# One step of a hybrid attention and matrix-memory layer on one core: stores issued from another DMA queue, and a longer way from fetch to cast

## The chip, the cores and the metric

The kernel runs on one core of one Trainium2 chip. The metric is the device time of one execution in microseconds (us); lower is better. The engines are TensorE (PE in the profile, with PEld for its weight loads), VectorE (DVE), ScalarE (ACT), GpSimd (POOL) and SyncE (SP), which here only issues transfers. A transfer (DMA) is an instruction in the queue of the engine that issues it: that engine waits for what the transfer needs, issues it and goes on. The kernel before issues from SyncE (SPq in the profile) and from ScalarE (ACTq).

## What is computed

One layer of a streaming encoder for two groups that share the weights: a prompt of 2048 rows and a sample group of 8 x 16 rows, 1024 wide, all in float32. Cut from the reference:

```python
h = rms_norm(x, norm_g[0])
z = h @ w_in
qa, ka, va, qb, kb, vb, ob, ib, fb = jnp.split(z, IN_SPLITS, axis=-1)
att = band_attention(qa, ka, va)      # 8 heads x 64; own chunk of 64 and 8 before, relative bias
att = rms_norm(att, g_att)
hb, (c1, n1, m1) = mlstm_sequence(qh, kh, vh, ig, lf, c0, n0, m0)   # 4 heads x 128, matrix memory
mlstm_out = head_rms_norm(hb) * g_mlstm * sigmoid(ob)
x = x + rms_norm(jnp.concatenate([att, mlstm_out], -1) @ w_out, norm_g[1])
u = rms_norm(x, norm_g[2]) @ w_up     # then a causal convolution of width 3, gelu(gate) * up
x = x + rms_norm(g @ w_down, norm_g[3])
```

The sample group attends to a cache of 512 keys and values and starts its matrix memory from a given state for each of its 8 sequences. Outputs are the rows and the new caches and states.

## The kernel before, in words

Every large product is made of three passes (`mm3`, lines 93 to 97): each float32 operand is split into a high part (a cast on ScalarE) and a low part (a subtraction on VectorE), and high x high, high x low and low x high are summed.

The kernel has two phases. In the **mixers' phase** TensorE works through the columns of `w_in` in 28 groups, 14 for each half of the prompt. ScalarE copies each result from TensorE's accumulators to a staging tile (L224, L226) and issues its store to DRAM (L239, L275). Between the pieces of this projection the work of the two mixers is woven in. At the end of the phase `project` (from L962) takes the mixed rows tile by tile through `w_out`, normalises them and adds the input. The **ConvFFN phase** follows, in three blocks of rows.

*How the weaving works.* Attention and matrix memory are streams of small generators, called units. A `Pipe` holds one stream: each call of `step` starts the next unit and moves every unit that is under way by one `yield`. `pump`, called after each piece of the projection with what that piece costs TensorE and VectorE, steps the two pipes in turn, at most two steps a call, until the planned VectorE time has caught up with a set share of the planned TensorE time. A `yield 0.0, 0.0` is a step without cost, and `bubble()` is an empty unit: it lets one step pass in which nothing new starts. So the distance in steps between two parts of a unit sets how much other work lies between them. From this order of emission, the framework fixes when the kernel is built in which order each engine gets its instructions and puts in all waits.

*The attention stream.* `load_head` (L321) fetches the bias, queries (L334) and keys (L337) of one head and one group of 512 rows into `raw` tiles, of which there are three; one step later it casts queries (L342) and keys (L346) and fetches the values (L351), and a step after that casts those (L355). Four `att_unit`s use them. `att_stream` starts the fetch of the next head ahead of the four units of the present one. Where it starts afresh (at the beginning, after the bias has been built, after each part of the sample group's attention) it starts the fetch, lets two empty units pass and then the fetch of the next head. At the end of a pair of heads `att_unit` stores 512 rows x 128 columns to `mixd` (L440).

*The matrix memory.* `prep_prompt` and `prep_sample` work out the gates; they store the running maxima (`md`, L582 and L623) and decays (`dd`, L583 and L624) to DRAM and load the decays back, broadcast (L585, L626). `mlstm` goes through a head in pairs of 128-row chunks; `finish_heads` (L633) ends a pair and stores it to `mixd` or `mixs` (L655), with two small GpSimd operations (L646, L647) in its middle. `mlstm_sample` takes the 8 states of a head two at a time: `batches` loads two (L769), prepares masked queries on GpSimd (`qz`, L771 and L774), multiplies (`cus`, L781 and L782), updates the states in place and stores them (L787). The tiles of these states share two buffers with the results that L655 stores, so a load waits until the store from two tiles before has landed.

*The sample group's attention* fetches keys (L847) and values (L897) of each sequence, GpSimd copies the own keys beside the cached ones (L848), ScalarE casts (L852, L901); the result goes to `atts` (L911). `project` ends each tile with an addition on GpSimd (L1027) and the store of `x2d` (L1028). GpSimd also masks the decay rows (L673), sets two corners of the bias (L326, L327) and takes square roots (L84).

Of the kernel before, what the change touches and what calls it, by code (L numbers as in the profile page):

```python
# [17 lines left out]
P = 128  # L18
# [26 lines left out]
def hymba_step(ctx: ExitStack, tc: tile.TileContext, I: dict, O: dict):  # L45
# [116 lines left out]
    def bubble():  # L162
        return iter([])
# [157 lines left out]
    def load_head(s):  # L321
        pair, kg, hh, h, nm = s.pair, s.kg, s.hh, s.h, s.nm
        if kg % 2 == 0:
            nb = pa.tile([P, 640], F32, tag="nb", name=f"nb{nm}", bufs=2)
            nc.sync.dma_start(nb, bias_src(h, P, 640))
            nc.gpsimd.memset(nb[0:64, 576:640], BIG)  # L326
            nc.gpsimd.memset(nb[64:128, 0:64], BIG)  # L327
            nbs[hh] = nb
        s.nb = nbs[hh]
        rows = slice(hh * 64, hh * 64 + 64)  # L330
        qr = raw_tile(f"qraw{nm}")[:, :512]
        krs = [raw_tile(f"kraw{nm}_{g}")[:, :512] for g in s.segs]
        for r in range(2):
            nc.sync.dma_start(qr[r * 64:r * 64 + 64, :], qTd[pair][kg][rows, :])  # L334
        for kr, g in zip(krs, s.segs):
            for r in range(2):
                nc.sync.dma_start(kr[r * 64:r * 64 + 64, :], kTd[pair][g][rows, :])  # L337
        yield 0.0, 0.0
        s.kh = pa.tile([P, 1024], F32R, tag="kh", name=f"kh{nm}", bufs=2)
        s.kl = pa.tile([P, 1024], F32R, tag="kl", name=f"kl{nm}", bufs=2)  # L340
        s.qs = pa.tile([P, 512], F32R, tag="qs", name=f"qs{nm}", bufs=2)
        nc.scalar.copy(s.qs, qr)  # L342
        nc.vector.tensor_tensor(s.qs[64:128], qr[64:128], s.qs[64:128], op=ALU.subtract)
        for si, kr in enumerate(krs):
            c = slice(si * 512, (si + 1) * 512)
            nc.scalar.copy(s.kh[:, c], kr)  # L346
            nc.vector.tensor_tensor(s.kl[:, c], kr, s.kh[:, c], op=ALU.subtract)
        new = [g for g in s.segs if g == kg or (h, g) not in vhl]
        vrs = [raw_tile(f"vraw{nm}_{g}")[:, :4 * DA].rearrange("p (a d) -> p a d", a=4) for g in new]
        for vr, g in zip(vrs, new):  # L350
            nc.sync.dma_start(vr, vd[h // 4][g][:, :, (h % 4) * DA:(h % 4 + 1) * DA])  # L351
        yield 0.0, 0.6 + 0.6 * len(krs)
        for vr, g in zip(vrs, new):
            t = pa.tile([P, 4, P], F32R, tag="vhl", name=f"vhl{nm}_{g}", bufs=4)
            nc.scalar.copy(t[:, :, 0:DA], vr)  # L355
            nc.vector.tensor_tensor(t[:, :, DA:P], vr, t[:, :, 0:DA], op=ALU.subtract)
            vhl[h, g] = t
        s.v = {g: vhl[h, g] for g in s.segs}
        if kg % 2:
            for g in s.segs:  # L360
                vhl.pop((h, g))
        yield 0.0, 0.34 * len(new)

    def att_unit(s, g2, j):
# [68 lines left out]
        for jj in range(4):  # L433
# [3 lines left out]
            st.rearrange("p a (h d) -> p a h d", h=2),  # L437
            ao.rearrange("p (a h d) -> p a h d", a=4, h=2),
            rinv.unsqueeze(3).broadcast_to([P, 4, 2, DA]), op=ALU.mult)
        nc.sync.dma_start(mixd[kg][:, :, pair * P:(pair + 1) * P], st)  # L440
        yield 0.43, 0.7

    def att_stream():

        ready = None
        while True:
            if ready is None:
                if not heads:
                    yield None
                    continue  # L450
                item = heads.popleft()
                if callable(item):
                    yield FLUSH
                    yield from item()
                    continue
                ready = item
                yield load_head(ready)
                yield bubble()
                yield bubble()
            cur, ready = ready, None  # L460
            if heads and not callable(heads[0]):
                ready = heads.popleft()
                yield load_head(ready)
            for g2 in range(2):
                for j in range(2):
                    yield att_unit(cur, g2, j)
# [80 lines left out]
    def prep_prompt(half):  # L547
        n = 8
        ig, lf, nlf = log_gates(1 + 8 * half, n, f"p{half}")
        f2 = lambda t: t.rearrange("p c h -> p (c h)")  # L550
        yield 0.3, 0.8
        a, b = cum_rows(f2(ig), f2(lf), f2(nlf), 32, tri, f"p{half}")
        ca = pm.tile([P, P], F32, tag="kw", name=f"cm{half}", bufs=2)[:32, :]
        nc.vector.tensor_tensor_scan(ca, a, a, NEG, op0=ALU.max, op1=ALU.max)
        yield 0.3, 0.4
        rt = ps_sm(f"rt{half}")
        transpose(rt[0:1, 0:32], ca[:, P - 1:P], 32)
        transpose(rt[0:1, 32:64], b[:, P - 1:P], 32)
        row = pm.tile([1, 2, n, HB], F32, tag="rowl", name=f"rowl{half}", bufs=1)
        nc.vector.tensor_copy(row.rearrange("p a c h -> p (a c h)"), rt[0:1, 0:64])  # L560
        o = 8 * half
        for h in range(HB):
            nc.vector.tensor_tensor_scan(mrow[:, o + 1:o + 9, h], row[:, 0, :, h], row[:, 1, :, h],
                                         mrow[:, o:o + 1, h], op0=ALU.max, op1=ALU.add)
        yield 0.3, 0.5
        mp = ps_sm(f"mp{half}")
        transpose(mp[0:32, 0:1], mrow[:, o:o + 8, :].rearrange("p c h -> p (c h)"), 1)
        mprev = small.tile([32, 1], F32, tag="mprev", name=f"mprev{half}")
        nc.vector.tensor_copy(mprev, mp[0:32, 0:1])
        yield 0.3, 0.8  # L570
        pk = pm.tile([P, P], F32, tag="kw", name=f"pk{half}", bufs=2)
        nc.vector.tensor_scalar(ca, ca, mprev, None, op0=ALU.max)
        nml = small.tile([32, 1], F32, tag="nml", name=f"nml{half}")
        nc.vector.tensor_scalar(nml, ca[:, P - 1:P], -1.0, None, op0=ALU.mult)
        nc.vector.tensor_copy(pk[0:32, :], a)
        nc.scalar.activation(pk[32:64, :], ca, AF.Exp, bias=mprev, scale=-1.0)
        nc.vector.tensor_tensor(b, b, ca, op=ALU.add)
        nc.scalar.activation(pk[64:96, :], b, AF.Exp, scale=-1.0)
        nc.scalar.activation(pk[96:128, :], a, AF.Exp, bias=nml)
        md = dt_([32, P], f"md{half}")  # L580
        dd = dt_([32, 1], f"dd{half}")
        nc.sync.dma_start(md, ca)  # L582
        nc.sync.dma_start(dd, pk[32:64, P - 1:P])  # L583
        dec = pm.tile([P, n, HB], F32, tag="dec", name=f"dec{half}", bufs=1)
        nc.sync.dma_start(dec, dd.rearrange("(c h) o -> o c h", c=n).broadcast_to([P, n, HB]))  # L585
        yield 0.0, 0.8
        cols = pack_columns(pk, "p")
        stab[half] = (md, dec, cols)
        yield 0.3, 0.8

    def prep_sample():
# [8 lines left out]
        a, b = cum_rows(f2(ig), f2(lf), f2(nlf), HB, trib, "s")  # L600
        yield 0.3, 0.8
        ms = small.tile([HB, DB], F32, tag="mss", name="mss")
        nc.sync.dma_start(ms, I["state_m"])
        ca = pm.tile([P, P], F32, tag="kw", name="cms", bufs=2)[:HB, :]
        nc.vector.tensor_tensor_scan(ca, reset, a, 0.0, op0=ALU.add, op1=ALU.max)
        v3 = lambda t: t.rearrange("p (b s) -> p b s", b=DB)
# [1 line left out]
        nc.vector.tensor_tensor(v3(ca), v3(ca), msb, op=ALU.max)  # L608
        mn_ = small.tile([HB, DB], F32, tag="mnew", name="mnew")
        nc.vector.tensor_tensor(mn_, v3(ca)[:, :, DS - 1], v3(b)[:, :, DS - 1], op=ALU.add)  # L610
        nc.sync.dma_start(O["m_sample"], mn_)
        pk = pm.tile([P, P], F32, tag="kw", name="pks", bufs=2)
        nc.vector.memset(pk, 0.0)
        nc.vector.tensor_copy(pk[0:HB, :], a)
# [5 lines left out]
            nc.scalar.activation(pk[o:o + HB, :], pk[o:o + HB, :], AF.Exp)  # L620
        md = dt_([HB, P], "mds")
        dd = dt_([HB, DB], "dds")
        nc.sync.dma_start(md, ca)  # L623
        nc.sync.dma_start(dd, v3(pk[32:32 + HB, :])[:, :, DS - 1])  # L624
        dec = pm.tile([P, HB, DB], F32, tag="decs", name="decs", bufs=1)
        nc.sync.dma_start(dec, dd.unsqueeze(0).broadcast_to([P, HB, DB]))  # L626
        yield 0.0, 0.8
        cols = pack_columns(pk, "s")
        stab["s"] = (md, dec, cols)
# [3 lines left out]
    def finish_heads(num, enm, og, h, nch, dst, name):  # L633
# [18 lines left out]
        for c in range(nch):  # L652
            nc.vector.scalar_tensor_tensor(num[:, c, 1:DH + 1], num[:, c, 1:DH + 1], f[:, c:c + 1], og[:, c, :],
                                           op0=ALU.mult, op1=ALU.mult)
        nc.sync.dma_start(dst, num[:, :, 1:DH + 1])  # L655

    def mlstm(h, half):
        md, dec, cols = stab[half]
# [21 lines left out]
        def chunk(s, c):  # L680
# [29 lines left out]
            finish_heads(num, cols[:, 2, r0:r0 + HB + 1:HB], s.og, h, 2,  # L710
                         mixd[sg][:, o:o + 2, 512 + h * DH:512 + (h + 1) * DH], s.nm)
            if half == 1 and s.pc == 3:
                nc.sync.dma_start(O["c_prompt"][h], cst[h])
            yield 0.0, 1.3

        pairs = [SimpleNamespace(pc=pc, t0=8 * half + 2 * pc, nm=f"{h}_{8 * half + 2 * pc}") for pc in range(4)]
# [9 lines left out]
    def mlstm_sample(h):  # L726
# [38 lines left out]
        def batches(bp):  # L765
# [18 lines left out]
                                           op0=ALU.mult, op1=ALU.add)  # L784
            nc.vector.tensor_tensor(cs, cs, dec[:, h, bs].unsqueeze(2).broadcast_to([P, 2, e]), op=ALU.mult)
            nc.vector.tensor_tensor(cs, cs, cu[:, :2 * e].rearrange("p (b e) -> p b e", b=2), op=ALU.add)
            nc.sync.dma_start(O["c_sample"][h][:, bs], cs)  # L787
            yield 0.85, 0.8

        def finish():  # L790
# [28 lines left out]
    def attention_sample(b0, b1):  # L819
# [74 lines left out]
        def values(b, kk):  # L894
# [13 lines left out]
            if kk == 4:  # L908
                so = pa.tile([P, 512], F32, tag="attT", name=f"so{b}", bufs=1)
                nc.vector.tensor_scalar(so, s.ot, s.rs, None, op0=ALU.mult)  # L910
                nc.sync.dma_start(atts[b], so)  # L911
            yield 0.64, 0.1

        yield queries()
# [47 lines left out]
    def project(tiles):  # L962
# [34 lines left out]
        for n_, s in enumerate(ss):  # L997
# [27 lines left out]
            rs = rsqrt_mean(ssq, D, f"n1_{t}", ssa)  # L1025
            nc.vector.scalar_tensor_tensor(m, m, rs, g1[0], op0=ALU.mult, op1=ALU.mult)
            nc.gpsimd.tensor_tensor(xr, m, xr, op=ALU.add)  # L1027
            nc.sync.dma_start(x2d[t], xr)  # L1028

# [224 lines left out]
                mems.append(lambda i=i: mlstm_sample(i))  # L1256
    for cost in out:
        pump(*cost)
    nc.sync.dma_start(O["m_prompt"], mrow[:, 16, :])


    p3, halo = ffn.p3, ffn.halo
# [431 lines left out]
```

## Time and profile before

| | us |
|---|---|
| median of three runs (lowest to highest) | 2796.95 (2793.69 to 2801.31) |
| the profiled execution, its own time | 2796.47 |
| its span, first to last instruction | 2794.8 |
| mixers' phase, about | 0 to 1330 |
| ConvFFN phase, about | 1330 to 2795 |

The mean granted clock of TensorE was 0.996 of full speed. In the rows of the profile, `a<-b` is the tile written and the tile read; L655 is a line of the kernel; `x32` a number of instructions. A row of waits names the engine and line that waited, what ended the wait, and then the total, the number of times and the longest. A row of the order of time begins with start and duration; an idle time before it stands in brackets with what ended it. A matmul's record lasts longer than the distance to the next one, since they are pipelined.

### The profile page before, as it was taken

Reading aid. Unit: us, or ns where it says so; the run is one execution under the profiler, and the core shown is the slowest. Engines: PE = TensorE matmul, PEld = TensorE weight load, DVE = VectorE, ACT = ScalarE, POOL = GpSimd, SP = SyncE. Lnnn points to the kernel's source line nnn. Section 1 sums busy time; section 2 is a strip of 40 time slices with the busy share of each in tenths; the row PEclk is TensorE's granted clock in tenths of the full one; section 3 lists DMA queues with packets and bytes.
Section 4 is the critical chain, followed back from the end, with each engine's and each line's share of the span. In section 5 each row is a group of like instructions: output and inputs, shape, how many; then the busy total and the mean of one; then the engine's idle time right before and its main releaser. Section 6 shows DMA issues by size and latency. Waiting matters only on the chain.

```text
span 2794.8 us, 47058 instructions
## 1 busy us (share of the span) xinstructions
PE 2729.5 (98%) x16587; PEld 2554.0 (91%) x16587; DVE 1877.1 (67%) x3442; ACT 1407.9 (50%) x2836; POOL 429.6 (15%) x876
## 2 busy tenths in 40 slices
PE   8899999999999999999999999999999999999998
PEld 7899999998899998888999988899999878999887
DVE  5244455655556668766999986457777864888855
ACT  4354555534356666534545555345455543555543
POOL 1000010211100002344211110011111210222221
PEclk9999999999999999999999999999999999999999
DMA  5534355557555456346655555644444774555685
GB/s 187 150 117 137 105 169 162 164 151 212 160 174 149 140 170 185 114 157 220 199 175 167 169 177 174 220 142 153 160 154 140 275 267 151 172 177 177 195 299 192
DMA packets 313419, 486.05 MB, mean 174 GB/s; under 512 B 55426, under 2 KB 150622, under 8 KB 313054
## 3 DMA queue, kind: packets, MB, share of 16 engines
q1 hardware_dynamic: 274590, 449.21, 50.7%
q10 hardware_dynamic: 38592, 33.83, 3.6%
q8 instruction: 130, 2.13, 0.3%
q14 instruction: 107, 0.88, 0.1%
HBM read 359.36 MB, written 126.70 MB: 174 GB/s over the span
## 4 chain that ended last, share of the span: by engine, by line
PE 55%; DVE 2%; DMA 1%; issue 1%; POOL 1%; ACT 1%; SPq 0%; DVEq 0%; POOLq 0%; ACTq 0%
PE uec L95 6%; PE uec L96 6%; PE uec L97 6%; PE dn L97 4%; PE dn L96 4%; PE dn L95 4%; PE ua L97 3%; PE ua L96 3%; PE ua L95 3%; PE dnm L97 2%; PE dnm L95 2%; PE dnm L96 2%; PE wo L97 2%; PE wo L95 2%; PE wo L96 2%; PE ub L96 1%
## 5 line engine op out<-in xcount | busy, mean ns | idle before, releaser
L95 PE MATMUL uec<-B,wuh 128*128 128x384 f32 (+1 forms) x720 | 234.9, 328 | 0.9 <-DVE uu L1418 0.7
L96 PE MATMUL uec<-B,wuh 128*128 128x384 f32 (+1 forms) x720 | 235.2, 327 | 0.0
L97 PE MATMUL uec<-B,wul 128*128 128x384 f32 (+1 forms) x720 | 234.0, 327 | 0.0
L1266 DVE TENSOR_TENSOR gl<-gr,gh 128x768 fp32r<-128x768 f32 (+3 forms) x141 | 121.7, 872 | 154.1 <-ACT gh L1265 145.7
L1265 ACT CAST gh<-gr 128x768 fp32r<-128x768 f32 (+3 forms) x141 | 102.0, 736 | 200.1 <-PE dn L96 184.3
L1265 ACT CAST wuh<-wu 128x512 fp32r<-128x512 f32 x255 | 141.7, 618 | 113.0 <-PE uec L96 100.9
L95 PE MATMUL dn<-wdh,gh 128*128 128x512 f32 x466 | 182.9, 393 | 2.2 <-DVE ug L1418 2.2
L96 PE MATMUL dn<-wdl,gh 128*128 128x512 f32 x466 | 184.1, 395 | 0.0
L97 PE MATMUL dn<-wdh,gl 128*128 128x512 f32 x466 | 168.3, 396 | 0.0
L1266 DVE TENSOR_TENSOR wul<-wu,wuh 128x512 fp32r<-128x512 f32 x255 | 164.7, 684 | 2.8 <-DMA x2d<-mx 2.8
L393 DVE CUSTOM_DVE_ANT_0 tmp<-s,nb 128x640 f32<-128x640 f32 (+4 forms) x128 | 94.4, 737 | 92.5 <-PE s L383 91.1
L95 PE MATMUL vo<-wi_h,hT 128*128 128x256 f32 x544 | 155.9, 287 | 0.6 <-DVE mt L199 0.6
L97 PE MATMUL vo<-wi_h,hT 128*128 128x256 f32 x544 | 156.4, 288 | 0.0
L96 PE MATMUL vo<-wi_l,hT 128*128 128x256 f32 x544 | 155.6, 286 | 0.0
L95 PE MATMUL qk<-hT,wi_h 128*128 128x384 f32 (+1 forms) x384 | 129.8, 338 | 8.7 <-ACT qk_st L224 7.7
L95 PEld LDWEIGHTS uec<-B,wuh 128*128 128x128 f32 x720 | 135.1, 188 | 2.7 <-DVE uu L1418 1.2
L96 PEld LDWEIGHTS uec<-B,wuh 128*128 128x128 f32 x720 | 135.4, 188 | 0.2
L97 PEld LDWEIGHTS uec<-B,wul 128*128 128x128 f32 x720 | 135.2, 188 | 0.0
L406 DVE TENSOR_TENSOR ptl<-pt,pth 128x640 fp32r<-128x640 f32 (+4 forms) x128 | 93.6, 737 | 54.9 <-ACT pth L405 53.7
L394 ACT ACTIVATE tmp<-tmp,mn 128x640 f32<-128x640 f32 (+4 forms) x128 | 97.6, 762 | 64.5 <-DVE mn L393 62.1
L96 PE MATMUL qk<-hT,wi_h 128*128 128x384 f32 (+1 forms) x384 | 129.1, 336 | 0.0
L97 PE MATMUL qk<-hT,wi_l 128*128 128x384 f32 (+1 forms) x384 | 128.7, 335 | 0.0
(411 smaller groups left out, 8876.7 us busy)
## 6 DMA issues: line engine op xcount, KB each, us to landing
wu<-in_w_up SPq DMA_DIRECT2D x220, 256.0 KB, 4.0
wu<-wsd SPq DMA_DIRECT2D x176, 256.0 KB, 4.8
wdr<-in_w_down SPq DMA_DIRECT2D x132, 256.0 KB, 5.1
gr<-gd SPq DMA_DIRECT2D x78, 384.0 KB, 4.2
wi_raw<-in_w_in SPq DMA_DIRECT2D x52, 512.0 KB, 3.9
wsd<-ws SPq DMA_DIRECT2D x88, 256.0 KB, 2.7
gd<-g SPq DMA_DIRECT2D x44, 384.0 KB, 3.5
kraw<-kTd SPq DMA_DIRECT2D x112, 128.0 KB, 3.4
```

What stands on the lines that cost most here:

```text
L95: nc.tensor.matmul(out, ah, bh, start=start, stop=False, skip_group_check=onto)
L96: nc.tensor.matmul(out, ah, bl, start=False, stop=False, skip_group_check=onto)
L97: nc.tensor.matmul(out, al, bh, start=False, stop=stop, skip_group_check=onto)
L393: nc.vector.tensor_tensor_reduce(o_, s_, b_, 1.0, 3e38, ALU.add, ALU.min, accum_out=mn)
L394: nc.scalar.activation(tmp[:, :n], tmp[:, :n], AF.Exp, bias=mn, scale=-1.0, accum_out=rsum[:, i % 4, hh:hh + 1])
L406: nc.vector.tensor_tensor(s.ptl[:, sl, qc], ptv, s.pth[:, sl, qc], op=ALU.subtract)
L1265: nc.scalar.copy(h, r)
L1266: nc.vector.tensor_tensor(l, r, h, op=ALU.subtract)
```

## The change

Two edits, all in the mixers' phase. Every store of that phase that SyncE issued goes to GpSimd's DMA queue, and so do three lines that load small tables: those of the decays, which read back what was just stored, and that of the sample's maxima. Counted in the profile of before these are 109 transfers: 16 of `mixd` from attention, 36 from `finish_heads`, 16 states of the sample group and 4 of the prompt, 8 of `atts`, 17 of `x2d`, and 12 small ones of the gates. The other loads stay on SyncE, and ScalarE's stores stay where they are. Second, `load_head` lets three steps pass instead of one between fetch and casts, and `att_stream` puts in four empty units instead of two where it starts afresh.

```diff
@@ load_head
                 nc.sync.dma_start(kr[r * 64:r * 64 + 64, :], kTd[pair][g][rows, :])
-        yield 0.0, 0.0
+        for _ in range(3):
+            yield 0.0, 0.0
@@ att_unit
-        nc.sync.dma_start(mixd[kg][:, :, pair * P:(pair + 1) * P], st)
+        nc.gpsimd.dma_start(mixd[kg][:, :, pair * P:(pair + 1) * P], st)
@@ att_stream
                 yield load_head(ready)
-                yield bubble()
-                yield bubble()
+                for _ in range(4):
+                    yield bubble()
@@ prep_prompt
-        nc.sync.dma_start(md, ca)
-        nc.sync.dma_start(dd, pk[32:64, P - 1:P])
+        nc.gpsimd.dma_start(md, ca)
+        nc.gpsimd.dma_start(dd, pk[32:64, P - 1:P])
...
-        nc.sync.dma_start(dec, dd.rearrange("(c h) o -> o c h", c=n).broadcast_to([P, n, HB]))
+        nc.gpsimd.dma_start(dec, dd.rearrange("(c h) o -> o c h", c=n).broadcast_to([P, n, HB]))
@@ prep_sample
-        nc.sync.dma_start(ms, I["state_m"])
+        nc.gpsimd.dma_start(ms, I["state_m"])
...
-        nc.sync.dma_start(O["m_sample"], mn_)
+        nc.gpsimd.dma_start(O["m_sample"], mn_)
...
-        nc.sync.dma_start(md, ca)
-        nc.sync.dma_start(dd, v3(pk[32:32 + HB, :])[:, :, DS - 1])
+        nc.gpsimd.dma_start(md, ca)
+        nc.gpsimd.dma_start(dd, v3(pk[32:32 + HB, :])[:, :, DS - 1])
...
-        nc.sync.dma_start(dec, dd.unsqueeze(0).broadcast_to([P, HB, DB]))
+        nc.gpsimd.dma_start(dec, dd.unsqueeze(0).broadcast_to([P, HB, DB]))
@@ finish_heads
-        nc.sync.dma_start(dst, num[:, :, 1:DH + 1])
+        nc.gpsimd.dma_start(dst, num[:, :, 1:DH + 1])
@@ mlstm
-                nc.sync.dma_start(O["c_prompt"][h], cst[h])
+                nc.gpsimd.dma_start(O["c_prompt"][h], cst[h])
@@ mlstm_sample, batches
-            nc.sync.dma_start(O["c_sample"][h][:, bs], cs)
+            nc.gpsimd.dma_start(O["c_sample"][h][:, bs], cs)
@@ attention_sample, values
-                nc.sync.dma_start(atts[b], so)
+                nc.gpsimd.dma_start(atts[b], so)
@@ project
-            nc.sync.dma_start(x2d[t], xr)
+            nc.gpsimd.dma_start(x2d[t], xr)
@@ hymba_step, after the projections
-    nc.sync.dma_start(O["m_prompt"], mrow[:, 16, :])
+    nc.gpsimd.dma_start(O["m_prompt"], mrow[:, 16, :])
```

## The prediction

> **What bounds the kernel now.** I read the page's first part, then the busy time by stage, then who waited for whom on TensorE and on SyncE's DMA queue, then the order of time around the longest gaps. The page:
>
> ```profile
> span 2794.8 us, 47058 instructions
> ...
> PE 2729.5 (98%) x16587; PEld 2554.0 (91%) x16587; DVE 1877.1 (67%) x3442; ACT 1407.9 (50%) x2836; POOL 429.6 (15%) x876
> ```
>
> TensorE is busy for 98% of the span, so no edit of transfers can win more than the time in which it stands still or runs slowly. The profiled execution took 2796.47 us, 1.67 more than its span and 0.48 below the median of the runs, 2796.95. I make the sum against 2796.47 and correct nothing for the half microsecond.
>
> Busy time by stage (window: its length, then busy PE, PEld, DVE, ACT, POOL; the granted clock; the share of the DMA engines; GB/s):
>
> ```profile
> 66.00:116.00 50.00, 41.96 (x226) 39.98 (x225) 13.58 (x50) 12.88 (x31) 1.63 (x7) 0.93 0.63 171
> 116.00:400.00 284.00, 284.00 (x2029) 281.07 (x2028) 135.82 (x301) 143.90 (x332) 7.73 (x29) 1.00 0.42 125
> 400.00:520.00 120.00, 118.36 (x894) 115.97 (x893) 69.45 (x167) 66.88 (x163) 13.26 (x41) 1.00 0.53 158
> 520.00:800.00 280.00, 264.73 (x1793) 247.84 (x1792) 151.89 (x422) 123.99 (x315) 42.97 (x129) 0.99 0.60 182
> 800.00:1040.00 240.00, 240.00 (x1885) 239.56 (x1884) 150.93 (x355) 152.65 (x372) 14.52 (x46) 1.00 0.52 152
> 1040.00:1330.00 290.00, 283.60 (x1558) 241.08 (x1557) 210.02 (x337) 148.69 (x353) 103.03 (x141) 0.99 0.52 171
> ```
>
> The mixers' phase ends at about 1330. From 116 to 400 and from 800 to 1040, prompt attention, projections and some matrix memory alone, TensorE loses nothing. It loses 8.04 us between 66 and 116, where attention and matrix memory start, 1.64 from 400 to 520, 15.27 from 520 to 800, where the sample group's attention and state run, and 6.40 in the output projection. The first three, 24.95 us, are what this change can reach. TensorE's waits from 66 to 800 (total, times, longest):
>
> ```profile
> PE qk L95 <- ACT qk_st L224: 7.7, 2, 4.4
> PE cus L781 <- DMA cs<-in_state_c: 5.6, 6, 1.9
> ...
> PE mas L760 <- DVE ad L644: 1.1, 1, 1.1
> ```
>
> I followed each back to a transfer that came late, as shown below. Now the waits of SyncE's DMA queue from 66 to 1100, the moved stores' own and the two that follow from them:
>
> ```profile
> SPq L440 <- DVE attst L436: 36.1, 9, 8.9
> ...
> SPq L655 <- DVE num L653: 27.5, 12, 11.8
> SPq L440 <- DVE wi_l L1176: 27.4, 4, 13.0
> ...
> SPq L655 <- DVE w L692: 8.2, 6, 5.4
> ...
> SPq L585 <- DMA dd<-pk: 7.0, 2, 3.5
> ...
> SPq L769 <- DMA out_c_sample<-cs: 24.6, 7, 4.4
> ...
> SPq L769 <- DMA mixd<-num: 7.4, 7, 1.8
> ```
>
> The first five rows are stores and the load of `dec` that the change takes off this queue: 106.2 us in which SyncE stood at one of them with loads behind it. The last two are loads of the sample state, L769, which wait for an earlier store to land because it still reads the buffer that they overwrite. They stay on SyncE.
>
> **The change part by part.**
>
> *First part, the load of `dec` at 735.* The store of `dd` and the load back of it go to GpSimd. In order of time:
>
> ```profile
> 734.46 0.20 POOL L848 COPY skr<-own 128x16 f32<-128x16 f32 x1
> ...
> 738.85 0.34 SPq L585 DMA_DIRECT2D dec<-dd  x1
> ...
> 739.28 0.86 SPq L847 DMA_DIRECT2D skr<-in_cache_k  x2
> ...
> 744.60 0.63 ACT L852 CAST skh<-skr 128x528 fp32r<-128x528 f32 x1 [9.14 <-DMA skr<-in_cache_k]
> ...
> 745.29 0.39 PE L95 MATMUL ss<-skh,zhl 128*128 128x264 f32 x1 [2.77 <-ACT skh L852]
> ```
>
> SyncE reaches L585 3.5 us early (the wait row above) and the sample keys are behind it. Without it they start 3.5 earlier, which covers the 2.77 for which TensorE stands. What follows that gap counts too:
>
> ```profile
> 104.00:108.00 4.00, 1.21 (x7) 0.90 (x6) 0.00 (x0) 0.00 (x0) 0.00 (x0) 1.00 1.02 265
> 108.00:112.00 4.00, 2.36 (x7) 2.36 (x8) 0.00 (x0) 1.16 (x4) 0.41 (x1) 0.54 0.72 191
> ...
> 746.00:750.00 4.00, 4.00 (x19) 4.00 (x18) 2.28 (x4) 2.55 (x6) 0.41 (x1) 0.57 0.54 157
> 750.00:754.00 4.00, 4.00 (x30) 4.00 (x30) 1.81 (x8) 1.31 (x4) 0.41 (x1) 1.00 0.76 210
> ```
>
> After a long gap the granted clock is 0.57 for four microseconds, in which 19 matmuls run where the next four hold 30. So the gap costs 4 x 0.43 = 1.72 more. This part: 2.77 + 1.72 = 4.49 gained.
>
> *Second part, the start of attention.* Here both edits act:
>
> ```profile
> 73.67 0.78 SPq L624 DMA_DIRECT2D dds<-pks  x1
> 74.80 0.51 SPq L334 DMA_DIRECT2D qraw<-qTd  x1
> ...
> 81.71 0.62 ACT L342 CAST qs<-qraw 128x512 fp32r<-128x512 f32 x1 [10.93 <-DMA qraw<-qTd]
> ...
> 82.76 0.44 PE L95 MATMUL qk<-hT,wi_h 128*128 128x384 f32 x1 [3.23 <-ACT qk_st L224]
> ```
>
> ScalarE sits 10.93 us at the cast of the first queries; the copies that empty TensorE's accumulators are queued behind it on the same engine, and TensorE stands 3.23. With `dds` away the second half of the queries starts up to 1.1 earlier, and with two more steps of the pipe between fetch and cast the accumulator copies go ahead of the cast. I take the whole 3.23. The other gap of this kind is the 4.4 of the wait row, at 105; there the 16 DMA engines were full (a share of 1.02 from 104 to 108), and the clock of 0.54 from 108 to 112 adds 4 x 0.46 = 1.84. The change lightens the queues but not the bytes, so the ends are 0 and 6.24 and I take half, 3.1.
>
> The two further steps cost nothing elsewhere: by the code the fetch of the next head enters six steps before that head's first attention step; its casts came one and two steps after the fetch and will come three and four after it, still ahead of the use, and from 800 to 1040 TensorE has no idle time by which casts could be late. What hides them is that cover of two steps; without it, each of 32 heads would expose a cast, 0.62. The two further empty steps come only where attention starts afresh and add no work.
>
> *Third part, the stores of `mixd`.* At 554 SyncE waits for a head's result, and the sample's values are next:
>
> ```profile
> 554.52 0.38 SPq L655 DMA_DIRECT2D mixd<-num  x1
> 555.07 1.61 SPq L742 DMA_DIRECT2D mvos<-vobd  x1
> ```
>
> The sample's first product, `mas`, then waits 1.1 (row above), which I count as gained. Most of the other 106.2 us delays loads that have time, as the full stages show.
>
> *Fourth part, what GpSimd pays.* No store is issued there now, so its price is bounded by rows:
>
> ```profile
> L655 SPq DMA_DIRECT2D mixd<-num x32: 360/377/1539, 382.6 to 1166.4; - x32
> ...
> DMA to landing us min/median/max: 2.2/3.5/4.3
> ...
> L647 POOL TENSOR_TENSOR mf<-ad,nhalf 128x2 f32<-128x2 f32 x32 | 25.3, 790 | 2.7
> ...
> L1027 POOL TENSOR_TENSOR mx<-mx 128x1024 f32<-128x1024 f32 x17 | 41.3, 2427 | 3.9 <-DVE mx L1026 3.9
> ```
>
> A store off a queue full of loads might land as the quickest does, 2.2 where the median is 3.5: 1.3 sooner. At the other end the store costs as much as the engine's longest instruction, 2.43, instead of SyncE's 0.38: 2.05 later. The nearest row is a short operation between semaphores, 0.79, so I take 0.79 - 0.38 = 0.4 later for each. It matters where a load waits for the landing and TensorE waits for the load:
>
> ```profile
> 707.93 0.34 SPq L787 DMA_DIRECT2D out_c_sample<-cs  x1
> 711.98 0.33 SPq L769 DMA_DIRECT2D cs<-in_state_c  x1
> ...
> 714.33 0.68 PE L781 MATMUL cus<-cs,qz 128*128 128x129 f32 x4 [1.94 <-DMA cs<-in_state_c]
> ```
>
> TensorE waited so 6 times: 6 x 0.4 = 2.4 lost. Behind a waiting store on GpSimd stand the memsets and copies of `qz`, the own keys (L848), the masks (L673) and the square roots (L84); GpSimd is busy 43 of the 280 us from 520 to 800, and the mean of these is under 1 us, so I cost them at nothing. Its cover is that idle time; if a store holds L848 for long, the first part's 4.49 goes. The 17 stores of `x2d` follow GpSimd's own addition L1027 directly and add no wait.
>
> *Sum:* 4.49 + 3.23 + 3.1 + 1.1 - 2.4 = 9.5 gained, 2796.47 - 9.5 = 2787.0 us.
>
> **The rivals.**
>
> *Slower.* The fourth part decides. Fourteen loads of the state wait for a store (the two L769 rows, 7 + 7). If each store lands later by more than (4.49 + 3.23 + 3.1 + 1.1) / 14 = 0.85, and no other work hides it, the gains are gone; from (11.9 + 8.4) / 14 = 1.45 the kernel is measurably slower. Midway from there to the bound, at 1.75, it is 14 x 1.75 - 11.9 = 12.6 slower: 2809. For it: SyncE already stands up to 4.4 for such a landing and loads of other streams are behind. Against: only 6 of 16 state products waited. The Trainium skill's page "SBUF — State Buffer", in its section "SBUF: two separate sides", speaks against the change: descriptors of GpSimd's DMAs are written by that engine, and it is locked out while VectorE runs copies in a two-port mode. No row of before can show it.
>
> *The wait moves along.* GpSimd stands for `dd` as SyncE did, and holds the own keys' copy (L848) that the cast L852 needs as well. Then 4.49 isn't gained: 2796.47 - 5.0 = 2791.5, no measurable change (here 0.3%, 8.4 us, is about what a measurement can tell). For it: GpSimd serves its queue in order, as SyncE does in the rows above. Against: the copy at 734.46 was done before the wait.
>
> *Only issue time is saved.* A queue costs the issuing engine time and nothing else, so the kernel saves SyncE's 32 x 0.377 = 12 us for `mixd` and the like; SyncE isn't the bound, so the time stays 2796.5. This is the rule of the Trainium skill's page "DMA: Bandwidth & Descriptors", section "Issuing engines are not separate DMA queues": other issuing engines save only sequencer time. The 106.2 us of waits at the head of SyncE's queue speak against it: they are no issue time.
>
> *All of it goes.* If every load comes early enough, the 24.95 us of idle go, and of the slow clock 50 x 0.07 + 280 x 0.01 = 6.3: 2765. Against: VectorE and ScalarE cause part of these gaps.
>
> **How the numbers follow.** Forecast 0.36; all of it 0.12; the wait moves along 0.18; only issue time 0.12; slower 0.22. So faster 0.48, the same 0.30, slower 0.22. The forecast's own range is 2774 to 2788: below by the other half of the gap, 3.1, and by stores that land 1.3 sooner instead of 0.4 later, 6 x 1.7 = 10.2; above by the bound of what counts as faster. The range that leaves out two in ten reaches from 2769, near the end of "all of it", to 2809, the slower rival's value.
>
> **What would show it.** In the profile after: no wait of SyncE at the lines 440, 655, 585, 787; a third DMA queue; the 10.93 at L342 down to a few microseconds and no PE gap before 85; no half clock at 746; `cus` waiting for `cs` not above some 8 us in total. I am wrong if GpSimd's stores take over 1.5 us each on its queue, if `cus` waits 15 us or more, or if new gaps open from 116 to 400 or 800 to 1040, where there are none.

## The result, and the profile after

The changed kernel takes 2824.61 us (median of 4 runs, 2822.60 to 2827.13) where the kernel before took 2795.32 beside it: a ratio of 1.0111, 95% interval 1.0099 to 1.0122. It is 29 us slower; the forecast was 9.5 us faster. The profiled execution took 2822.6, its span is 2820.9.

The page of the kernel after, its first part and the new queue:

```profile
span 2820.9 us, 47133 instructions
...
PE 2739.7 (97%) x16587; PEld 2557.9 (91%) x16587; DVE 1873.5 (66%) x3442; ACT 1407.5 (50%) x2836; POOL 498.9 (18%) x985
...
q0 software_dynamic: 7312, 22.13, 2.2%
```

The work is the same, 16587 matmuls, and 109 instructions moved to GpSimd (876 to 985). Busy time by stage of the kernel after, columns as in the prediction:

```profile
66.00:116.00 50.00, 39.70 (x213) 37.22 (x212) 12.14 (x43) 11.54 (x26) 5.71 (x14) 0.93 0.61 175
116.00:400.00 284.00, 283.62 (x2027) 281.61 (x2026) 132.93 (x299) 143.26 (x334) 10.95 (x32) 1.00 0.40 122
400.00:520.00 120.00, 115.30 (x843) 111.07 (x842) 67.53 (x172) 64.13 (x161) 20.70 (x51) 0.99 0.54 160
520.00:800.00 280.00, 259.26 (x1737) 243.56 (x1736) 148.81 (x411) 120.11 (x302) 65.31 (x166) 0.96 0.55 170
800.00:1040.00 240.00, 238.03 (x1841) 235.41 (x1840) 142.19 (x332) 144.70 (x353) 24.75 (x60) 1.00 0.52 155
```

TensorE stands still for longer in each of these stages, by 2.3, 0.4, 3.1, 5.5 and 2.0 us, and from 520 to 800 the granted clock fell from 0.99 to 0.96. Even the stage from 800 to 1040, full before, has holes.

The waits of SyncE's queue in the kernel after, 66 to 1100 (a line number above 337 is one higher than before):

```profile
SPq L1170 <- DVE wi_l L1177: 86.8, 23, 13.5
...
SPq L669 <- PE ma L701: 62.2, 14, 9.6
...
SPq L770 <- DMA mixd<-num: 26.3, 8, 6.6
...
SPq L770 <- DMA out_c_sample<-cs: 15.8, 7, 4.0
```

The stores are gone from it, as meant. But rid of the stores SyncE runs on to the next load and waits there. Its waits for a buffer of weights (L1170) rose from 52.2 to 86.8, and those for the landing of a `mixd` store from 7.4 to 26.3. The row of before for the first of these is

```profile
SPq L1169 <- DVE wi_l L1176: 52.2, 25, 9.1
```

The order of time of SyncE's and GpSimd's transfers in the kernel after, around 553, shows one such wait:

```profile
552.04 0.33 SPq L743 DMA_DIRECT2D mvos<-vobd  x1
555.62 0.33 SPq L770 DMA_DIRECT2D cs<-in_state_c  x1
```

```profile
553.10 0.80 POOL L656 DMA_DIRECT2D mixd<-num  x1 [0.27 <-issue]
```

SyncE is at the load of the state at 552.4, before the store that must free its buffer has been issued on the other queue, and stands there for 3.2 us with the rest of its queue behind it. This was my first theory of the loss; the experiments below put all that the queue does at 7.5 us (p1), a quarter of the loss.

What TensorE waits for in the kernel after, 66 to 800:

```profile
PE cus L782 <- DMA cs<-in_state_c: 6.3, 3, 4.5
PE qk L95 <- ACT qk_st L226: 5.8, 1, 5.8
...
PE pkTs L67 <- ACT pks L621: 2.9, 1, 2.9
...
PE cus L782 <- POOL skr L849: 2.0, 1, 2.0
```

### The profile page after: what moved, and what is told of

It reads as the page before. It is cut to its first block, busy times and chain, and to the rows that moved or that the text cites. A ratio compares the mean times of both kernels' runs of the same rounds, so it can differ in the third digit from the quotient of the medians.

```text
span 2820.9 us, 47133 instructions
## 1 busy us (share of the span) xinstructions
PE 2739.7 (97%) x16587; PEld 2557.9 (91%) x16587; DVE 1873.5 (66%) x3442; ACT 1407.5 (50%) x2836; POOL 498.9 (18%) x985
## 4 chain that ended last, share of the span: by engine, by line
PE 52%; DVE 4%; DMA 2%; issue 1%; POOL 1%; ACT 1%; SPq 0%; DVEq 0%; POOLq 0%; ACTq 0%
PE uec L95 6%; PE uec L96 6%; PE uec L97 6%; PE dn L97 4%; PE dn L95 4%; PE dn L96 4%; PE ua L97 3%; PE ua L96 3%; PE ua L95 3%; PE dnm L95 2%; PE dnm L97 2%; PE dnm L96 2%; PE ub L96 1%; PE ub L97 1%; PE ub L95 1%
```

## The experiments

The kernel before ran beside each group on the same chip; its medians were 2795.3, 2795.9, 2790.5, 2793.6 and 2791.4, so only ratios within a group are compared. Where microseconds are given for a ratio, they are the ratio less one, times 2795.

**Which edit.** First the two edits apart, then the whole change with one group of stores taken back.

`e1`: all moved stores on GpSimd, the waiting steps as before.

> The kernel before with the stores on GpSimd's queue alone; fetch and casts one step apart as before. Theory A (the stores: a load of the state waits on SyncE for a store on GpSimd, and GpSimd's own work stands behind waiting stores): nearly the whole loss, 2815 to 2825 us. Theory C (the two further steps): the time of before or a little less, 2785 to 2797. Theory D (any edit of this kind re-lines the order, and 10 to 30 us of gaps come and go with it): anything between 2795 and 2825.

`e2`: the other edit alone, stores on SyncE.

```diff
-        yield 0.0, 0.0
+        for _ in range(3):
+            yield 0.0, 0.0
...
-                yield bubble()
-                yield bubble()
+                for _ in range(4):
+                    yield bubble()
```

> The kernel before with the two further steps alone; all stores on SyncE. Theory A: 2790 to 2797 us, with the first gap at 79 to 83 us (3.2) gone. Theory C: 2815 to 2825. Theory D: off the time of before by 5 to 20 us either way, with gaps at new places.

`e3`: the change, with attention's store back on SyncE.

```diff
-        nc.gpsimd.dma_start(mixd[kg][:, :, pair * P:(pair + 1) * P], st)
+        nc.sync.dma_start(mixd[kg][:, :, pair * P:(pair + 1) * P], st)
```

> The changed kernel with the 16 stores of attention (mixd<-attst) back on SyncE. If GpSimd's standing at these stores is the cause (196 us of waits at L441, with masks, own keys and square roots behind them): most of the loss comes back, 2795 to 2805 us. If the state's chain of store and load is the cause: 2818 to 2826, unchanged.

`e4`: the change, with the stores of `finish_heads` and of the states back on SyncE.

```diff
-        nc.gpsimd.dma_start(dst, num[:, :, 1:DH + 1])
+        nc.sync.dma_start(dst, num[:, :, 1:DH + 1])
...
-            nc.gpsimd.dma_start(O["c_sample"][h][:, bs], cs)
+            nc.sync.dma_start(O["c_sample"][h][:, bs], cs)
```

> The changed kernel with the stores of finish_heads (mixd<-num, mixs<-nums) and of the sample's states (out_c_sample<-cs) back on SyncE, in one queue with the loads that wait for them. If that chain is the cause (42 us of waits of SyncE at L770 against 32 before, TensorE 6.3 at cus and longer gaps around it): 2795 to 2808 us. If attention's stores are: 2818 to 2826, unchanged.

| kernel | median us | ratio, 95% interval |
|---|---|---|
| e1, stores only | 2807.41 | 1.0045 (1.0027 to 1.0063) |
| e2, steps only | 2814.46 | 1.0073 (1.0052 to 1.0094) |
| e3, the change without attention's stores | 2825.84 | 1.0112 (1.0090 to 1.0134) |
| e4, the change without the stores of the chain of states | 2811.24 | 1.0056 (1.0035 to 1.0078) |

e1 lies between what theories A and C allow and e2 just under theory C's 2815; only theory D, which allows nearly anything, has room for both. Both edits lose, and 1.0045 and 1.0073 add up to the change's 1.0111 within their intervals. By e3 and e4 it seemed that the stores' loss sat in the two kinds that share buffers with the state loads. So each edit was cut in two.

**The halves.** `e5` has the two further steps between fetch and casts alone, `e6` the two further empty steps alone, `e7` the stores of `finish_heads` and of the states alone (36 and 16; its expectation counts too many), `e8` all other moved stores alone; the edits are the parts of those above.

> Of the two halves of the steps edit, only the two further steps between a head's fetch and its casts; empty steps and stores as before. Both halves together cost 19 us (2814.5 against 2795.3). Theory Y, the casts that come two steps later are the cost, for each of 32 heads: 2814, and attention's last unit ends some 28 us later, at 1213. Theory B, the empty steps at the three fresh starts are the cost: 2795 here. Theory R, any edit that moves work by a step re-deals the order of the later work, and the cost belongs to neither half: the two halves do not add up to 19, and each may be anywhere from -5 to +25.

> The other half alone: four empty steps instead of two where attention starts afresh (three times in the kernel), casts one step after the fetch as before, stores as before. Theory Y: 2795, no change. Theory B: 2814. Theory R: a change of either sign that, added to the one of the yields alone, does not give 19.

> Only the two stores of the chain of sample state on GpSimd, those of finish_heads and of c_sample (48 + 16 + 16 or so stores); the other moved stores and the steps as before. Theory C, SyncE no longer stands at the store but runs on to the next load of state, which stands there until the store on the other queue lands, with other loads behind: all of the stores' cost is here and the gain of the gates' stores is not, so 2807 or a few more, up to 2812. Rival D, cost spread over all moved stores: about 2800. Rival E, the cost is an interplay with the attention's stores: 2795 to 2798.

> The moved stores without that chain: attention's, the gates' small ones and the load of dec, sample attention's and the rest on GpSimd, finish_heads and c_sample on SyncE, no further steps. Theory C: no cost is left and the gap before the sample keys (2.77 and the slow clock after it, 4.5 together) is gone, so 2790 to 2795. Rival D: 2802. Rival E: 2795 to 2800.

| kernel | median us | ratio, 95% interval |
|---|---|---|
| e5, later casts | 2813.78 | 1.0068 (1.0055 to 1.0082) |
| e6, more empty steps | 2817.53 | 1.0079 (1.0066 to 1.0093) |
| e7, the two kinds of the chain | 2805.26 | 1.0039 (1.0027 to 1.0051) |
| e8, all other stores | 2811.05 | 1.0057 (1.0044 to 1.0070) |

Nothing adds up any more. The halves of the steps lose 1.0068 and 1.0079 apart and 1.0073 together; those of the stores 1.0039 and 1.0057 apart and 1.0045 together. So it was chance that the two edits of the first table added up. Theory Y had no cost for e6 and theory B none for e5; both fail. e8 should have gained by the theory that all loss was in the chain, and lost 16 us. What is left is the theory called R and O in the expectations: the framework fixes each engine's order when the kernel is built, and each of these edits makes it deal that order anew. When the 16587 matmuls of a trace are listed by the tiles that they write and read (buffer numbers left out), the list of e1 has 2290 lines of difference from that of the kernel before, e8 1780, e7 906 and e2 3426, though no edit touches a matmul.

**The order held.** So the order was taken out of the comparison. At the end of the emission every instruction that stays on its engine gets an edge to the one that stood ahead of it there in the kernel before. The edge binds the order and is no wait; only the moved stores find their own place in GpSimd's queue. `ORDER` is the list read from the kernel before.

```diff
+    for engine in ("PE", "DVE", "Activation", "SP", "Pool"):
...
+            if prev is not None:
+                tc.add_manual_dep(ins, prev.name, edge, reason="order of before")
+            prev = ins
```

`p1` is e1 so bound, `p7` is e7, `p8` is e8. `x1` is the reverse: stores on SyncE, but TensorE, VectorE, ScalarE and GpSimd bound to the order of e1; SyncE's own order is left free. `c0`, run later, is the kernel before bound to its own order. In the traces the same list of matmuls, and such a list of the operations of VectorE, ScalarE and GpSimd, has no line of difference between the kernel before and c0, p1, p7 or p8, and none between e1 and x1.

> All moved stores on GpSimd, no further steps, but TensorE, VectorE, ScalarE, SyncE and GpSimd get the instructions they keep in exactly the order in which they stand in the kernel before; only where the stores stand in GpSimd's queue is free. (Left free, the same edit changes the order: some 5,500 lines of difference on TensorE, and it took 2807.4.) Theory O, the cost is the order that the framework deals anew when a store changes its queue, not the queue: 2786 to 2796, with the gap before the sample keys gone as first forecast. Theory M, the cost is made on the chip, by loads of state that wait at the head of SyncE's queue for a store on the other queue: 2805 to 2812 here too.

> Only the stores of finish_heads and of c_sample on GpSimd, every other instruction in the order of the kernel before. Left free this took 2805.3. Theory O: 2793 to 2798, as before. Theory M: 2803 to 2808, and loads of state (L769) that wait for a landing hold SyncE for about as long as in the kernel after, 42 us in all where it was 32.

> The other moved stores alone (attention's, the gates', sample attention's, the output projection's) on GpSimd, every other instruction in the order of the kernel before. Left free this took 2811.1. Theory O: 2788 to 2794, the gain of the gap before the sample keys (4.5) and some of the first gap, nothing lost. Theory M for these stores: 2807 to 2813.

> The other way round: all stores stay on SyncE, but TensorE, VectorE, ScalarE and GpSimd get their instructions in the order that they have in the kernel with all stores on GpSimd (2807.4); SyncE's own order is free. Theory O: 2803 to 2815, the cost without its queue. Theory M: 2793 to 2798, as before, since the queue is that of before. In between, some 2800: half of it is order.

> The kernel before with every instruction bound to its own order and nothing moved: the binding adds no instruction and no wait, so ratio 1.000 within 0.001 by every theory; its profile stands beside those of the same chip.

| order | stores on SyncE | stores on GpSimd |
|---|---|---|
| of the kernel before | c0: 0.9999 (0.9991 to 1.0008) | p1: 1.0027 (1.0016 to 1.0038) |
| of e1 | x1: 1.0057 (1.0043 to 1.0070) | e1: 1.0045 (1.0027 to 1.0063) |

The order of e1 costs 16 us with every store on the queue of before; the queue costs 7.5 us with the order of before; in e1's order the queue makes no difference that these intervals show. Held to the order of before, p7 has 1.0025 (1.0015 to 1.0036) where e7 had 1.0039, and p8 has 1.0009 (1.0000 to 1.0019) where e8 had 1.0057. For e8, then, some four fifths of the loss are order. x1 is where theory O had it, and p8 is far nearer to O, though without the gain that O promised; p7, 7 us slower, is at the lower end of theory M, and p1 lies between the two. Both causes are there. For all stores together and for those of e8 the order is the larger; for the two kinds of e7 the queue is, 0.25 of the 0.39%.

**Is it these edits or any edit?** `n2` has one empty step more than the kernel before at the three fresh starts of attention, `n3` one less, which is the opposite of the change.

```diff
                 yield bubble()
+                yield bubble()
                 yield bubble()
```

> Three empty steps instead of two at the three fresh starts of attention, nothing else (four took 21.6 us more). Theory S, any edit by which the order is dealt anew loses, whatever its sense: 2803 to 2818 on a chip where the kernel before takes 2796 (ratio 1.003 to 1.008). Theory T, the cost is that of more empty steps: half of 21.6, ratio 1.004. (This run alone doesn't tell them apart; the next one does.)

> One empty step instead of two, the opposite of the change. Theory S: slower again, ratio 1.003 to 1.008. Theory T: the sign turns, ratio 0.996 to 1.000.

n2: 2818.32 us, 1.0091 (1.0078 to 1.0105). n3: 2802.57 us, 1.0030 (1.0018 to 1.0041). One step more loses as much as two more, and one less loses too: in the time there is no dose and no sign. Theory T fails in both; theory S has n3 at the lower end of its range and n2 above it. With these, all ten kernels besides the change itself whose order was dealt anew (e1 to e8, n2, n3) are slower, by 0.3 to 1.1%.

Where n2 loses can be read beside c0, on the same chip. The first matmul of the output projection, attention's last `s`, and the first matmul of the ConvFFN phase, in c0:

```profile
1052.34 0.48 PE L95 MATMUL wo<-wo,mt 128*128 128x512 f32 x1
...
1182.43 0.31 PE L383 MATMUL s<-kl,qs 128*128 128x320 f32 x1
...
1320.06 0.34 PE L95 MATMUL ua<-B,wuh 128*128 128x384 f32 x1
```

and in n2:

```profile
1062.75 0.48 PE L95 MATMUL wo<-wo,mt 128*128 128x512 f32 x1
...
1210.55 0.31 PE L383 MATMUL s<-kl,qs 128*128 128x320 f32 x1
...
1343.13 0.34 PE L95 MATMUL ua<-B,wuh 128*128 128x384 f32 x1
```

The projections end 10.4 us later, the output projection takes 280.4 instead of 267.7 us, 12.7 more, and that is the loss: 23.1 of 23.9 in the span. Attention ends 28 us later, so more of it lies in the output projection.

The place is not the same in all. The change's steps alone, e2, start the output projection 2.7 us later than the kernel before and take 287.9 us for it instead of 267.1, 20.9 more; e5 and e6, one half of that edit each, take 284.3 and 289.3. The stores alone, e1, e7 and e8, start it 8.4, 4.1 and 10.4 us later and take 267.3 to 270.6 for it. The kernel after has both, its first `wo` at 1075.1, 19 us later, and 273.8 for the output projection. So the kernels with more steps have something in common after all. In e2, e5, e6 and n2 the last `s` of attention comes 148 to 156 us after the first `wo`, in the kernel before 129 and in n3, with one step less, 131. That this later end of attention is what the steps cost is a reading of the place; no run holds the rest and moves attention alone.

In the projections the loss of n2 is in the stage of the sample group, whose windows for c0

```profile
520.00:800.00 280.00, 266.63 (x1829) 249.18 (x1828) 154.56 (x428) 125.49 (x318) 44.99 (x134) 1.00 0.61 185
800.00:1040.00 240.00, 240.00 (x1888) 239.53 (x1887) 153.01 (x359) 154.44 (x374) 15.39 (x46) 1.00 0.50 149
```

stand against these of n2:

```profile
520.00:800.00 280.00, 259.87 (x1721) 242.12 (x1720) 143.17 (x408) 117.54 (x300) 40.55 (x125) 0.97 0.58 172
800.00:1040.00 240.00, 237.68 (x1844) 235.05 (x1843) 143.88 (x336) 147.76 (x355) 12.88 (x42) 1.00 0.51 150
```

6.8 us more idle and a clock of 0.97, so 108 matmuls fewer in the same 280 us. In n2, where no store was moved, TensorE waits for states longer than in the kernel after, 9.6 us against 6.3 (c0: 4.7):

```profile
PE cus L782 <- DMA cs<-in_state_c: 9.6, 5, 4.1
```

**Where the gain of the gates' stores went.** `p9` moves only `md`, `dd`, `dec` and their counterparts of the sample to GpSimd, order held.

```diff
-        nc.sync.dma_start(md, ca)
-        nc.sync.dma_start(dd, pk[32:64, P - 1:P])
+        nc.gpsimd.dma_start(md, ca)
+        nc.gpsimd.dma_start(dd, pk[32:64, P - 1:P])
...
-        nc.sync.dma_start(dec, dd.rearrange("(c h) o -> o c h", c=n).broadcast_to([P, n, HB]))
+        nc.gpsimd.dma_start(dec, dd.rearrange("(c h) o -> o c h", c=n).broadcast_to([P, n, HB]))
```

> Only the gates' small stores and the two loads of the decays on GpSimd, every other instruction bound to the order of the kernel before. My forecast's first part and the first half of its second hold: 4.5 + 3.2 gained, ratio 0.9972. Rival, the gap before the sample keys is refilled by the next late thing, as the profile with all stores moved has it (2.2 of the 2.9 us left at 738): ratio 0.999 to 1.000.

Measured: 2793.70 us, 1.0001 (0.9992 to 1.0010), which rules out the 0.9972 and agrees with the rival. SyncE's transfers around 735 in c0, and its waits for `dd`:

```profile
730.76 0.33 SPq L582 DMA_DIRECT2D md<-cm  x1
731.19 1.25 SPq L583 DMA_DIRECT2D dd<-pk  x1
733.63 0.38 SPq L664 DMA_DIRECT2D mb<-md  x1
737.66 0.34 SPq L585 DMA_DIRECT2D dec<-dd  x1
738.09 0.86 SPq L847 DMA_DIRECT2D skr<-in_cache_k  x2
```

```profile
SPq L585 <- DMA dd<-pk: 4.9, 2, 3.6
```

SyncE's and GpSimd's in p9, and the wait of SyncE's queue that is new:

```profile
737.32 0.38 SPq L664 DMA_DIRECT2D mb<-md  x1
737.80 0.88 SPq L847 DMA_DIRECT2D skr<-in_cache_k  x2
```

```profile
732.47 0.59 POOL L582 DMA_DIRECT2D md<-cm  x1 [1.97 <-DVE nml L574]
...
738.04 0.57 POOL L585 DMA_DIRECT2D dec<-dd  x1 [1.19 <-DMA dd<-pk]
```

```profile
SPq L664 <- DMA md<-cm: 6.6, 1, 6.6
```

The wait for `dd` at L585 is gone, and in its place SyncE stands 6.6 us at L664, which reads back `md`, stored by GpSimd. The sample keys behind it start at 737.80, where c0 has 738.09.

**Which store of the chain.** `p5` moves the stores of `finish_heads` alone, `p6` those of the states alone, order held.

> Only the 36 stores of finish_heads on GpSimd, every other instruction bound to the order of the kernel before. Both kinds together took a ratio of 1.0025, and the loads of the state that wait for these landings rose from 7.8 to 26.8 us, those that wait for the states' own stores only from 23.5 to 29.9. Theory L, those waits are the cost: ratio 1.002 here, and the row of L769 behind mixd at 20 us or more. Rival I, the cost is GpSimd's issue of each store, 0.3 us more than SyncE's, spread over both kinds by their number: 1.0017 here too but 1.0008 for the other kind, and no rise of that row.

> Only the 16 stores of the sample group's states on GpSimd, every other instruction bound to the order of the kernel before. Theory L: 1.0000 to 1.0007, the row of L769 behind out_c_sample at 24 to 30 us. Rival I: 1.0008. If the two kinds do not add up to 1.0025, the cost is neither's alone.

p5: 2792.80 us, 1.0006 (0.9998 to 1.0015). p6: 2793.85 us, 1.0013 (1.0003 to 1.0022). SyncE's waits at the state loads, in c0 and in p5:

```profile
SPq L769 <- DMA out_c_sample<-cs: 23.5, 7, 4.4
SPq L769 <- DMA mixd<-num: 7.8, 7, 2.1
```

```profile
SPq L769 <- DMA mixd<-num: 26.0, 7, 5.7
SPq L769 <- DMA out_c_sample<-cs: 22.3, 7, 4.4
```

The row rose as theory L wanted, by 18 us, and the time did not: L's 1.002 lies outside the interval, and so does the 1.0017 of rival I. So these 18 us, with SyncE's waits at L655 gone in exchange, cost at most some 4 us. p6's interval holds what either theory said of the time; its row behind `out_c_sample` rose to 35.6, above the 24 to 30 of theory L. The two give 1.0019 together, within p7's interval; how that small loss arises stays open.

## Why the prediction was wrong, point by point

*The step that failed* is the one the whole sum took for granted, and that it states in its second part: "The two further steps cost nothing elsewhere", the empty steps "add no work". They add no work, and they cost 20 us (e2, 1.0073). Since they add no operation to any engine and move none to another queue, what they change is the order of the rest. The same holds for the stores: x1 shows 16 us of order without any store moved. I read the idle times of one order and summed what each edit does to them, as if the rest stayed where it was. The lesson stood in my own text on the kernel: the framework fixes the order when the kernel is built. In no rival did I ask what the edit does to that. What makes the new orders worse is shown only as far as the place: for the added steps mostly the output projection, which attention reaches further into (20.9 of the 24.5 us by which e2's span is longer), for the stores mostly the time before it. Why all ten lose stays open; whether some other order would win was not tried.

*First part, 4.49 for the load of `dec`.* Wrong, and not only by the order: p9 holds it and gains nothing. The wait at L585 goes, but the load that follows in the queue, L664, needs `md`, whose store also went to GpSimd. My rival "the wait moves along" had the mechanism and put it on the wrong engine. TensorE's gap before the sample keys, 2.08 in c0,

```profile
743.46 0.39 PE L95 MATMUL ss<-skh,zhl 128*128 128x264 f32 x1 [2.08 <-ACT skh L852]
```

is still 1.04 in p9:

```profile
743.81 0.39 PE L95 MATMUL ss<-skh,zhl 128*128 128x264 f32 x1 [1.04 <-ACT skh L852]
```

And the 1.72 for the slow clock is no fixed price of this gap: in c0, where it lasts 2.08 instead of 2.77, the clock stays at 1.00.

```profile
740.00:744.00 4.00, 1.92 (x11) 1.59 (x10) 0.56 (x1) 0.63 (x1) 0.41 (x1) 1.00 0.71 254
744.00:748.00 4.00, 3.64 (x25) 3.38 (x24) 2.34 (x5) 2.49 (x6) 0.41 (x1) 1.00 0.47 133
```

In the kernel after no such wait before the sample keys' product is left, but one of 4.5 us stands before a `cus` at 731 instead.

*Second part, 3.23 and half of the gap at 105.* TensorE's two gaps at the start of attention, in c0:

```profile
83.45 0.45 PE L95 MATMUL qk<-hT,wi_h 128*128 128x384 f32 x1 [4.05 <-ACT qk_st L224]
110.50 0.44 PE L95 MATMUL qk<-hT,wi_h 128*128 128x384 f32 x1 [3.11 <-ACT qk_st L224]
```

and in p9:

```profile
81.79 0.44 PE L95 MATMUL qk<-hT,wi_h 128*128 128x384 f32 x1 [1.66 <-ACT qk_st L224]
103.98 0.44 PE L95 MATMUL qk<-hT,wi_h 128*128 128x384 f32 x1 [3.51 <-ACT qk_st L226]
```

The stores' part of the first gap is real, 2.4 us; the second stays. The steps do their part too: e2 is 45.17 us busy from 66 to 116 where the kernel before was 41.96. In the kernel after nothing of it is left: in the new order TensorE waits 2.9 us for `pkTs` and then the 5.8 of the row above, and the stage has 39.70 busy.

*Third part, 1.1 for `mas`.* No run settles it: in c0, with queues and order as before, TensorE's wait for `ad` is not there either.

*Fourth part, what GpSimd pays.* The size of one issue was right. The stores' price in the kernel after:

```profile
L656 POOL DMA_DIRECT2D mixd<-num x32: 722/788/807, 389.3 to 1199.9; - x32
...
DMA to landing us min/median/max: 2.3/3.4/6.6
```

0.788 for SyncE's 0.377 is 0.41 more (forecast 0.4), the states' stores took 0.541, and the median landing, 3.4, is that of before, 3.5. The forecast loss of 2.4 at `cus` is about right with the order held: TensorE's wait there is 4.7 in c0 and 6.6 in p1. The slower rival, 14 loads that wait for later landings, is not what happened: by the median landings came no later, though the longest took 6.6 instead of 4.3. The loads wait longer because SyncE reaches them sooner, as at 552.4 above, and p5 shows how little that costs. What I put at nothing, GpSimd's own work behind a waiting store, shows in one row of the kernel after, the 2.0 of `cus` behind the copy L849. GpSimd stood 196.1 us at attention's stores there. But e3, with these back on SyncE, is no faster than the change, and p8, which moves them with the order held, is 1.0009.

*The rival "only issue time"*, no change, came nearest of all to what the queue alone does: p1 is 1.0027, p8 1.0009, p9 1.0001. The Trainium skill's page "DMA: Bandwidth & Descriptors" says in its section "Issuing engines are not separate DMA queues" that another issuing engine saves only the sequencer's time for issuing. The runs with the order held agree in that nothing was gained; that p1 is 7.5 us slower goes beyond it. The 106.2 us of waits that I set against it bought nothing: SyncE's waits moved to the next load in its queue.

*What I said would show it.* Right: no wait at the four lines, a third queue, ScalarE's 10.93 before the first cast of queries down to 0.94, a clock of 1.00 from 746 to 750, the `cus` wait below 8 us (6.3), stores under 1.5 us each, next to nothing new from 116 to 400 (0.4 us). These show that the edits did locally what they should. Wrong: TensorE still has gaps before 85, the 2.9 for `pkTs` and 0.6 at 83. The sign that spoke against the forecast was the last: 238.03 busy from 800 to 1040, where there had been 240.00.

## What to carry to other kernels

Where a framework fixes the order of all engines when it builds the kernel, an edit of one queue or one empty step can be an edit of the whole order. Compare the built orders first, and test the edit with the order held, before a trace of one order is used to price it. A store that moves to another queue takes its wait along to whichever load in the old queue reads back what it stored or overwrites what it still reads; look for that load before the wait is counted as gained. A wait at the head of a transfer queue is a loss only if TensorE ends up waiting for something behind it: here 18 us more of it at one load made a difference of at most some 4.

## What the runs showed of the hardware

Issuing a store took GpSimd 0.54 us for the states and 0.79 us for `mixd` from `finish_heads`, against 0.34 and 0.38 on SyncE; the latter landed 3.4 us after issue by the median, against 3.5. All 32 of `mixd` lay between 0.722 and 0.807 us, so the lock-out of GpSimd by VectorE that I cited from the Trainium skill's page "SBUF — State Buffer", section "SBUF: two separate sides", left no mark on these times; whether VectorE ran such copies beside them is not shown. A gap of TensorE is followed by a slow clock in some cases only: not after 2.06 us before the sample keys' product in p1 nor after 2.08 in c0, but after 2.21 in p7, where the clock was 0.50 from 742 to 744, and in the kernel after, where it stood 4.5 us before a `cus` at about 731, the clock was 0.72 and then 0.50:

```profile
728.00:732.00 4.00, 1.16 (x5) 1.19 (x6) 0.00 (x0) 0.00 (x0) 0.00 (x0) 0.72 0.37 108
732.00:736.00 4.00, 4.00 (x17) 2.82 (x16) 2.14 (x10) 0.40 (x2) 0.64 (x2) 0.50 0.09 33
```
